# A row sum on one core: one block of 128 rows for each partition in place of two blocks of 15 and 113

## The chip, the core and the metric

The kernel runs on one core of one Trainium2 chip. The core has several engines that run side by side and wait for each other through semaphores (counters): VectorE (DVE in the profile), ScalarE (ACT), GpSimd (POOL) and SyncE (SP), which here only issues transfers. Transfers between HBM, the chip's large memory, and the core's on-chip memory with its 128 partitions are carried out by 16 DMA engines. The metric is the time of one execution on the device, in microseconds (us). The kernel before takes 160.44 us, the median of three runs (160.27 to 160.67).

## The reference

The input x has 32 x 512 rows of 1024 float32 numbers, 16384 rows and 67.1 MB in all. Each row is summed and divided by 1024:

```python
def reference(x: np.ndarray, divisor: float) -> np.ndarray:
    return (np.sum(x, axis=-1) / divisor).astype(np.float32)
```

The output is 16384 numbers, 0.07 MB. The work is reading x once.

## The kernel before

**Which partition has which rows.** With 16384 rows and 128 partitions, each partition sums J = 128 rows. The kernel divides x into two regions. The first region, the first 128 x 15 rows of x (`x_first`, F = 15), gives each partition 15 consecutive rows, so the pieces of two neighbouring partitions begin 15 rows (60 KB) apart. The second region, the rest, gives each partition W = 113 consecutive rows, which begin 113 rows (452 KB) apart. Of these 113 rows, M = 97 are called `main` (`x_main`) and L = 16 are called `last` (`x_last`). Lines 52 to 60 say this, and the same for the output.

**The loads.** A load takes some rows for all partitions at once: for each partition one contiguous piece of up to 16 rows (64 KB). The bulk loads go in turn to three buffers, `bulk0` to `bulk2`, of 16 rows each. In order they have 2, 16, 16, 16, 16, 16 and 15 rows of `main`, then the 15 rows of `first`, then the 16 rows of `last` in pieces that do not end at row boundaries: 10.625 rows and 3.66 rows into bulk buffers (loads 8 and 9), and 1.3 rows (`pa`) and 0.4 rows (`pb`) into small buffers of their own. Numbered from 0, load 6 is the 15-row one of `main` and load 7 is the one of `first`.

**Who issues them.** All transfers are issued by SP, in one queue. The first two are issued ahead of the rest (line 116). Load 2 waits for load 0 to land. From load 3 on (lines 140 to 144), load k waits until the engines have finished with load k-3, which lay in the same buffer. `pa` and `pb` follow without a wait (lines 145 and 146). Then SP waits for POOL and issues the store of the 15 results of `first` (line 148), waits for the semaphore of `pa` to reach 17, which ScalarE brings about close to the end, and issues the store of the 97 results of `main` (line 150). At the end it waits for two more signals (line 237), issues the store of the 16 results of `last` (line 238), waits for the two early stores, clears the semaphores and waits for the last store to land (line 244).

**Who sums.** VectorE reduces all rows of a load with one instruction (line 215), except in loads 6 and 7: there the table says how many rows ScalarE takes from the end of the load, 4 of 15 and 6 of 15, each with one instruction that copies a row to scratch and adds it up (line 183).

```python
    main = [(2, 0)] + [(16, 0)] * 5 + [(15, 4)]
    first = [(15, 6)]
```

The rows of `last` are shared out by hand between VectorE, which adds the two halves of a row to each other while summing (line 205), and ScalarE; both apply the division as a scale. The results of `main` and `first` are still unscaled; POOL multiplies each of the two sets with one instruction (lines 157 and 161), as soon as the loads concerned have been summed.

Of the kernel before, what the change touches and what calls it, by code (L numbers as in the profile page):

```python
# [35 lines left out]
def kernel(  # L36
# [6 lines left out]
    nc = tc.nc  # L43
    nc.at_finalize(start_loads_at_once)
    xf = x.flatten_outer_dims()
    N, D = xf.shape
    P = nc.NUM_PARTITIONS
    scale = 1.0 / float(divisor)
    J = N // P
    assert J * P == N  # L50

    F, L = 15, 16
    M = J - F - L
    W = M + L
    x_first = bass.AP(tensor=x.tensor, offset=0, ap=[[F * D, P], [1, F * D]])
    x_main = bass.AP(tensor=x.tensor, offset=P * F * D, ap=[[W * D, P], [1, M * D]])
    x_last = bass.AP(tensor=x.tensor, offset=P * F * D + M * D, ap=[[W * D, P], [1, L * D]])
    o_first = bass.AP(tensor=out.tensor, offset=0, ap=[[F, P], [1, F]])
    o_main = bass.AP(tensor=out.tensor, offset=P * F, ap=[[W, P], [1, M]])
    o_last = bass.AP(tensor=out.tensor, offset=P * F + M, ap=[[W, P], [1, L]])  # L60

    def room(name, *shape):
        return nc.alloc_sbuf_tensor(name, [P, *shape], F32).ap()
# [5 lines left out]
    bulk = [room(f"bulk{i}", 16 * D) for i in range(3)]  # L69
# [7 lines left out]
    pa, row14 = tail[:, 256 : 256 + ends[3] - ends[2]], tail[:, 255 : 256 + D - c14]  # L77
    pb = room("pb", 512)[:, : D - c15 + 2]
    part = room("part", 1)
    res0 = room("res0", F)  # L80
    res = room("res", M)
    fin = room("fin", L)
    junk = [nc.alloc_psum_tensor(f"junk{i}", [P, D], F32).ap() for i in range(4)]
# [3 lines left out]
    loads = []  # L87
    sems = {}

    def sem(name):  # L90
        sems[name] = nc.alloc_semaphore(name)
        return sems[name]

    in_bulk = [sem(f"in_bulk{i}") for i in range(3)]
    in_pa, in_pb = (sem(f"in_{n}") for n in ("pa", "pb"))
    out_first, out_main = sem("out_first"), sem("out_main")
    dve, act, pool = sem("by_dve"), sem("by_act"), sem("by_pool")
    done = sem("done")
    landed = nc.alloc_semaphore("landed")

    main = [(2, 0)] + [(16, 0)] * 5 + [(15, 4)]
    first = [(15, 6)]
    assert sum(r for r, _ in first) == F and sum(r for r, _ in main) == M
    for rows_of, src, dst in ((main, x_main, res), (first, x_first, res0)):
        j = 0
        for rows, on_act in rows_of:
            t = bulk[len(loads) % 3][:, : rows * D]
            loads.append((t, in_bulk[len(loads) % 3], src[:, j * D : (j + rows) * D], on_act, dst[:, j : j + rows]))
            j += rows
    for k in range(2):  # L110
        t = bulk[len(loads) % 3][:, : ends[k + 1] - ends[k]]
        loads.append((t, in_bulk[len(loads) % 3], x_last[:, ends[k] : ends[k + 1]], 0, None))
# [9 lines left out]
    done_dve, done_act = {}, {}  # L122
# [21 lines left out]
        nc.sync.dma_start(out=t, in_=src).then_inc(s, 16)  # L144
    nc.sync.dma_start(out=pa, in_=x_last[:, ends[2] : ends[3]]).then_inc(in_pa, 16)
    nc.sync.dma_start(out=pb[:, : D - c15], in_=x_last[:, ends[3] : ends[4]]).then_inc(in_pb, 16)
    nc.sync.wait_ge(pool, 3)
    nc.sync.dma_start(out=o_first, in_=res0).then_inc(out_first, 16)
    nc.sync.wait_ge(in_pa, 17)
    nc.sync.dma_start(out=o_main, in_=res).then_inc(out_main, 16)  # L150

# [2 lines left out]
    k = len(main) - 1  # L154
    nc.gpsimd.wait_ge(dve, done_dve[k])
    nc.gpsimd.wait_ge(act, done_act[k])
    nc.gpsimd.tensor_scalar_mul(out=res, in0=res, scalar1=scale).then_inc(pool)  # L157
    k += len(first)
    nc.gpsimd.wait_ge(act, done_act[k])
    nc.gpsimd.wait_ge(dve, done_dve[k])  # L160
    nc.gpsimd.tensor_scalar_mul(out=res0, in0=res0, scalar1=scale).then_inc(pool)  # L161


    (t8, s8, *_), (t9, s9, *_) = loads[-2:]
# [21 lines left out]
    for k, (t, s, src, on_act, dst) in enumerate(loads[:-2]):  # L186
        rows = t.shape[1] // D
# [23 lines left out]
    for k, (t, s, src, on_act, dst) in enumerate(loads[:-2]):  # L211
        m = t.shape[1] // D - on_act
        nc.vector.wait_ge(s, arrived[k])
        rows = t[:, : m * D].rearrange("p (r d) -> p r d", d=D)
# [21 lines left out]

    nc.sync.wait_ge(done, 2)
    nc.sync.dma_start(out=o_last, in_=fin).then_inc(landed, 16)
    for s in (out_main, out_first):
        nc.sync.wait_ge(s, 16)  # L240
    ids = [s.num for s in sems.values()]
    assert max(ids) - min(ids) + 1 == len(ids)
    nc.sync.sem_clear(range(min(ids), max(ids) + 1))
# [36 lines left out]
```

## Time and profile before

| what | value |
|---|---|
| median of three runs | 160.44 us |
| span of the profiled execution, first to last instruction | 159.3 us |
| time outside the span, by the median | 1.1 us |
| VectorE busy | 116.7 us (73%) |
| ScalarE busy | 18.6 us (12%) |
| POOL busy | 1.0 us (1%) |
| read from HBM | 67.11 MB, 422 GB/s over the span |
| share of the 16 DMA engines' span with packets under way | 98.1% |

The profiled execution's own time is not given apart from its span, so the median stands for it. The page of a profile lists, for each group of instructions, the engine and line, how often and how long it ran, and what ended the idle time before it. "Releaser" is what an instruction waited for last. In a timeline a line reads: start, duration, engine, line, operation, output and input with their shapes, count, and in brackets the engine's idle time before it and its releaser. A load's landing is not an instruction; it shows as the start of the first instruction that waited for it. A packet is a piece of a transfer that one DMA engine moves; a bulk load has one packet for each partition.

### The profile page before, as it was taken

Reading aid. Unit: us, or ns where it says so; the run is one execution under the profiler, and the core shown is the slowest. Engines: PE = TensorE matmul, PEld = TensorE weight load, DVE = VectorE, ACT = ScalarE, POOL = GpSimd, SP = SyncE. Lnnn points to the kernel's source line nnn. Section 1 sums busy time; section 2 is a strip of 40 time slices with the busy share of each in tenths; the row PEclk is TensorE's granted clock in tenths of the full one; section 3 lists DMA queues with packets and bytes.
Section 4 is the critical chain, followed back from the end, with each engine's and each line's share of the span. In section 5 each row is a group of like instructions: output and inputs, shape, how many; then the busy total and the mean of one; then the engine's idle time right before and its main releaser. Section 6 shows DMA issues by size and latency. Waiting matters only on the chain.

```text
span 159.3 us, 144 instructions
## 1 busy us (share of the span) xinstructions
DVE 116.7 (73%) x32; ACT 18.6 (12%) x35; POOL 1.0 (1%) x7
## 2 busy tenths in 40 slices
DVE  0500009999499994999949999499989990399296
ACT  3000000000000000000000000000009100392196
POOL 0000000000000000000000000000000001000000
DMA  8996996996996997979969969969996999889894
GB/s 296 494 527 263 527 527 263 527 527 263 527 527 263 527 444 346 527 313 477 527 263 527 527 263 527 494 278 463 494 494 262 478 494 494 350 350 525 344 401 154
DMA packets 2160, 67.18 MB, mean 422 GB/s; under 512 B 624, under 2 KB 752, under 8 KB 880
## 3 DMA queue, kind: packets, MB, share of 16 engines
q1 hardware_dynamic: 2160, 67.18, 98.1%
HBM read 67.11 MB, written 0.07 MB: 422 GB/s over the span
## 4 chain that ended last, share of the span: by engine, by line
DMA 67%; DVE 30%; another core or an unknown queue 1%; issue 0%
DMA bulk<-in_x_dram 67%; DVE res L215 29%; DVE bulk L205 1%; DVE tail L205 0%; DVE pb L205 0%; DVE fin L205 0%
## 5 line engine op out<-in xcount | busy, mean ns | idle before, releaser
L215 DVE TENSOR_REDUCE res<-bulk 128x16 f32<-128x16384 f32 (+3 forms) x8 | 110.0, 13754 | 37.7 <-DMA bulk<-in_x_dram 37.7
L183 ACT ACTIVATE junk<-bulk 128x1024 f32<-128x1024 f32 (+1 forms) x16 | 15.6, 973 | 137.2 <-DMA bulk<-in_x_dram 137.2
L205 DVE CUSTOM_DVE_ANT_0 bulk<-bulk 128x512 f32<-128x512 f32 (+1 forms) x9 | 5.5, 665 | 3.1 <-DMA bulk<-in_x_dram 3.1
L183 ACT ACTIVATION_READ_ACCUMULATOR junk<-bulk 128x1 f32 x16 | 3.0, 187 | 0.0
L183 ACT ACT_TABLE_LOAD x1 | 1.3, 1283 | 1.9 <-PEq L119 1.9
L157 POOL TENSOR_SCALAR res<-res 128x97 f32<-128x97 f32 x1 | 0.5, 465 | 129.8 <-DVE res L215 129.8
L205 DVE DVE_READ_ACCUMULATOR2_ANT fin<- 128x1 f32 x10 | 0.8, 82 | 0.0
L183 ACT ACTIVATE junk<-tail 128x737 f32<-128x737 f32 x1 | 0.8, 789 | 0.0
L205 DVE CUSTOM_DVE_ANT_0 bulk<-bulk,part 128x192 f32<-128x192 f32 x1 | 0.4, 420 | 0.3 <-DMA bulk<-in_x_dram 0.3
L205 DVE CUSTOM_DVE_ANT_0 tail<-tail 128x304 f32<-128x304 f32 x1 | 0.5, 476 | 0.0
L205 DVE CUSTOM_DVE_ANT_0 pb<-pb 128x209 f32<-128x209 f32 x1 | 0.4, 379 | 0.1
L161 POOL TENSOR_SCALAR res<-res 128x15 f32<-128x15 f32 x1 | 0.3, 262 | 15.6 <-DVE res L215 15.6
L183 ACT ACTIVATION_READ_ACCUMULATOR junk<-tail 128x1 f32 x1 | 0.2, 187 | 0.0
L153 POOL MEMSET pb<- 128x2 f32 x1 | 0.1, 99 | 1.5 <-POOLq L119 1.5
L261 POOL MEMSET const-bfloat16-1.0<- 128x1 bf16 x1 | 0.1, 101 | 0.0
L261 POOL MEMSET const-uint8-127<- 128x1 uint8 x1 | 0.1, 101 | 0.0
L261 POOL MEMSET const-float32-0.0<- 128x1 f32 x1 | 0.1, 98 | 0.2 <-issue 0.2
L261 POOL MEMSET const-float32-1.0<- 128x1 f32 x1 | 0.1, 98 | 0.0
L205 DVE DVE_READ_ACCUMULATOR2_ANT pb<- 128x1 f32 x1 | 0.1, 84 | 0.0
L205 DVE DVE_READ_ACCUMULATOR2_ANT part<- 128x1 f32 x1 | 0.1, 83 | 0.0
## 6 DMA issues: line engine op xcount, KB each, us to landing
bulk<-in_x_dram SPq DMA_DIRECT2D x2, 7680.0 KB, 39.3
bulk<-in_x_dram SPq DMA_DIRECT2D x1, 5440.0 KB, 32.0
bulk<-in_x_dram SPq DMA_DIRECT2D x1, 1872.0 KB, 23.5
bulk<-in_x_dram SPq DMA_DIRECT2D x1, 1024.0 KB, 4.6
tail<-in_x_dram SPq DMA_DIRECT2D x1, 672.0 KB, 24.7
pb<-in_x_dram SPq DMA_DIRECT2D x1, 208.0 KB, 24.8
bulk<-in_x_dram SPq DMA_DIRECT2D x5, 40.8
out_dram<-res SPq DMA_DIRECT2D x1, 48.5 KB, 1.6
```

The costliest lines, as they stand in the source:

```text
L153: nc.gpsimd.memset(pb[:, D - c15 :], 0.0).then_inc(pool)
L157: nc.gpsimd.tensor_scalar_mul(out=res, in0=res, scalar1=scale).then_inc(pool)
L161: nc.gpsimd.tensor_scalar_mul(out=res0, in0=res0, scalar1=scale).then_inc(pool)
L183: nc.scalar.activation(scratch, src, COPY, scale=by, accum_out=dst).then_inc(count)
L205: return nc.vector.tensor_tensor_reduce(out=src[:, :h], in0=src[:, :h], in1=src[:, h:], scale=by, scalar=ahead, op0=ADD, op1=ADD, accum_ou ...
L215: nc.vector.reduce_sum(out=dst[:, :m], in_=rows, axis=AX).then_inc(dve)
L261: nc = _bacc.Bacc("TRN2", target_bir_lowering=False, num_devices=1)
```

## The change

The two regions become one. Each partition owns J = 128 consecutive rows of x, and the pieces of two neighbouring partitions begin 128 rows (512 KB) apart in every load. Of the 128 rows the first M = 112 are `main` and the last L = 16 are `last`. The bulk loads of `main` have 2, then six times 16, then 14 rows; ScalarE takes 4 rows of the last 16-row load (load 6) and 5 rows of the 14-row load (load 7). The four pieces of `last` keep their sizes and their order.

With one set of 112 results there is one scaling on POOL in place of two, after load 7, and one early store in place of two. The store waits for POOL's semaphore at 2 (the clearing of two columns of `pb`, and the scaling) and then for the semaphore of `pa`, as the store of `main` did. The buffer `res0` and the semaphore `out_first` go.

```diff
-    F, L = 15, 16
-    M = J - F - L
-    W = M + L
-    x_first = bass.AP(tensor=x.tensor, offset=0, ap=[[F * D, P], [1, F * D]])
-    x_main = bass.AP(tensor=x.tensor, offset=P * F * D, ap=[[W * D, P], [1, M * D]])
-    x_last = bass.AP(tensor=x.tensor, offset=P * F * D + M * D, ap=[[W * D, P], [1, L * D]])
-    o_first = bass.AP(tensor=out.tensor, offset=0, ap=[[F, P], [1, F]])
-    o_main = bass.AP(tensor=out.tensor, offset=P * F, ap=[[W, P], [1, M]])
-    o_last = bass.AP(tensor=out.tensor, offset=P * F + M, ap=[[W, P], [1, L]])
+    L = 16
+    M = J - L
+    x_main = bass.AP(tensor=x.tensor, offset=0, ap=[[J * D, P], [1, M * D]])
+    x_last = bass.AP(tensor=x.tensor, offset=M * D, ap=[[J * D, P], [1, L * D]])
+    o_main = bass.AP(tensor=out.tensor, offset=0, ap=[[J, P], [1, M]])
+    o_last = bass.AP(tensor=out.tensor, offset=M, ap=[[J, P], [1, L]])
...
-    main = [(2, 0)] + [(16, 0)] * 5 + [(15, 4)]
-    first = [(15, 6)]
-    assert sum(r for r, _ in first) == F and sum(r for r, _ in main) == M
-    for rows_of, src, dst in ((main, x_main, res), (first, x_first, res0)):
-        j = 0
-        for rows, on_act in rows_of:
-            t = bulk[len(loads) % 3][:, : rows * D]
-            loads.append((t, in_bulk[len(loads) % 3], src[:, j * D : (j + rows) * D], on_act, dst[:, j : j + rows]))
-            j += rows
+    main = [(2, 0)] + [(16, 0)] * 5 + [(16, 4), (14, 5)]
+    assert sum(r for r, _ in main) == M
+    j = 0
+    for rows, on_act in main:
+        t = bulk[len(loads) % 3][:, : rows * D]
+        loads.append((t, in_bulk[len(loads) % 3], x_main[:, j * D : (j + rows) * D], on_act, res[:, j : j + rows]))
+        j += rows
...
-    nc.sync.wait_ge(pool, 3)
-    nc.sync.dma_start(out=o_first, in_=res0).then_inc(out_first, 16)
+    nc.sync.wait_ge(pool, 2)
     nc.sync.wait_ge(in_pa, 17)
     nc.sync.dma_start(out=o_main, in_=res).then_inc(out_main, 16)
...
-    k += len(first)
-    nc.gpsimd.wait_ge(act, done_act[k])
-    nc.gpsimd.wait_ge(dve, done_dve[k])
-    nc.gpsimd.tensor_scalar_mul(out=res0, in0=res0, scalar1=scale).then_inc(pool)
...
-    for s in (out_main, out_first):
-        nc.sync.wait_ge(s, 16)
+    nc.sync.wait_ge(out_main, 16)
```

More of the change, by code (lines that the diff above doesn't have):

```diff
@@ L79 @@
     part = room("part", 1)
-    res0 = room("res0", F)
     res = room("res", M)
@@ L95 @@
     in_pa, in_pb = (sem(f"in_{n}") for n in ("pa", "pb"))
-    out_first, out_main = sem("out_first"), sem("out_main")
+    out_main = sem("out_main")
     dve, act, pool = sem("by_dve"), sem("by_act"), sem("by_pool")
```

## The prediction

> **What bounds the kernel now.** I read the page's opening, its DMA queue and its chain first, because they say whether the time lies in transfers or in an engine.
>
> ```profile
> span 159.3 us, 144 instructions
> DVE 116.7 (73%) x32; ACT 18.6 (12%) x35; POOL 1.0 (1%) x7
> ...
> q1 hardware_dynamic: 2160, 67.18, 98.1%
> HBM read 67.11 MB, written 0.07 MB: 422 GB/s over the span
> ...
> DMA 67%; DVE 30%; another core or an unknown queue 1%; issue 0%
> ```
>
> The 16 DMA engines hold packets for 98.1% of the span, VectorE (DVE) works for 73% of it. The chain puts 30% on DVE, so the second view must say whether that share is work that the loads wait for. The timeline of DVE shows when each load had landed: the start of the instruction behind it, with the idle time before it in brackets.
>
> ```profile
> 4.61 2.29 DVE L215 TENSOR_REDUCE res<-bulk 128x2 f32<-128x2048 f32 x1 [4.61 <-DMA bulk<-in_x_dram]
> 23.93 17.22 DVE L215 TENSOR_REDUCE res<-bulk 128x16 f32<-128x16384 f32 x1 [17.04 <-DMA bulk<-in_x_dram]
> ...
> 62.65 17.22 DVE L215 TENSOR_REDUCE res<-bulk 128x16 f32<-128x16384 f32 x1 [2.15 <-DMA bulk<-in_x_dram]
> 81.98 17.22 DVE L215 TENSOR_REDUCE res<-bulk 128x16 f32<-128x16384 f32 x1 [2.11 <-DMA bulk<-in_x_dram]
> 101.57 17.22 DVE L215 TENSOR_REDUCE res<-bulk 128x16 f32<-128x16384 f32 x1 [2.38 <-DMA bulk<-in_x_dram]
> 119.83 1.03 ACT L183 ACTIVATE junk<-bulk 128x1024 f32<-128x1024 f32 x1 [116.64 <-DMA bulk<-in_x_dram]
> 119.83 11.89 DVE L215 TENSOR_REDUCE res<-bulk 128x11 f32<-128x11264 f32 x1 [1.04 <-DMA bulk<-in_x_dram]
> ...
> 137.99 9.76 DVE L215 TENSOR_REDUCE res<-bulk 128x9 f32<-128x9216 f32 x1 [6.26 <-DMA bulk<-in_x_dram]
> ...
> 150.82 0.49 DVE L205 CUSTOM_DVE_ANT_0 bulk<-bulk 128x320 f32<-128x320 f32 x1 [3.08 <-DMA bulk<-in_x_dram]
> ...
> 155.28 0.42 DVE L205 CUSTOM_DVE_ANT_0 bulk<-bulk,part 128x192 f32<-128x192 f32 x1 [0.29 <-DMA bulk<-in_x_dram]
> ```
>
> Every reduction starts because its load has landed; DVE idles 2.1 us or more before each large one. A 16-row load lands every 19.33 us at best (62.65 to 81.98), 19.59 us at worst (81.98 to 101.57): 8.39 MB in 19.33 us is 434 GB/s. And the queue never runs dry: with three buffers, SyncE (SP) issues a load when the third load before it is consumed, 17.2 us after its landing, when the load in flight has some 2 us left and a whole one stands behind it. The DVE share of the chain is the way back from a DMA issue to the reduction that freed its buffer, not a delay of the queue. So the time is the start to the first landing (4.60 us), the stream from there to 155.28 us, and a tail of 4.0 us. The last view, SP's own waits, gives the end:
>
> ```profile
> SPq L244 <- SPq L244: 0.8, 1, 0.8
> SPq L238 <- DVE fin L205: 0.6, 1, 0.6
> SPq L243 <- DMA out_dram<-res: 0.2, 1, 0.2
> ```
>
> SP waits last for the landing of the final store (0.8 us after the clear of the semaphores), and that store waits for DVE.
>
> The sum starts from the span of 159.3 us. The runs shown have a median of 160.44 (160.27 to 160.67); the 1.1 us around the span is carried unchanged, so I add changes to 160.44.
>
> **The change, part by part.**
>
> *Boundaries of the loads.* Bytes and count stay: ten bulk loads, then pa and pb. Loads 0 to 5 keep their rows. Load 6 has 16 rows for 15, so it lands one row later, 1.21 us (19.35/16), at 121.0 us. DVE reduces 12 of them instead of 11; by its two shapes (16 rows 17.22 us, 11 rows 11.89 us) a row is 1.07 us, so 12.95 us, done at 134.0 us instead of 131.7. SP issues the last bulk load (buffer 0) behind that, then pa and pb: 2.3 us later, at about 134.0, 134.4 and 134.9 us by the issue times of before. The queue needs them when the load before ends, at 150.8 us: 16 us of cover, so 0. If that cover were gone the price would be the 2.3 us. Load 7 has 14 rows for 15; the rows landed by then are 112 both times, so it lands at 138.0 us as before. DVE still takes 9 of its rows (9.76 us, done at 147.8, before the 150.8 at which it is needed); ScalarE (ACT) takes 5 instead of 6, 1.0 us less inside an idle stretch. 0.
>
> *One scaling, one early store.* The two POOL multiplications (97 columns 0.465 us, 15 columns 0.262 us) become one of 112 columns, 0.50 us by their slope, between 147.8 and 148.3 us. SP waits for it (pool at 2), then for row 14's head (in_pa at 17, met at 156.85 us): it has 8.5 us in hand, so the new order of waits delays no queued store. What goes from SP is the issue of the 15-column store at 148.2 us (0.35 us, with SP idle around it) and one wait at the end, under the landing of the last store. Its 128 packets of 60 B lay behind pb in the same queue; by the packet records each took 0.011 us, eight to an engine, 0.09 us. They write while slower engines still read pb. Saved: between 0 and 0.09 us; I take 0. The remaining early store writes 448 B a partition for 388 B: the packets of 388 B took 0.024 us, so 0.03 us more over an engine's eight packets, and the wait for that landing ends 0.8 us before the last one. 0.
>
> *The addresses.* This is what is left, and it touches every byte. Before, a load of the main part takes 64 KB from each of 128 places 452 KB apart (113 rows of 4 KB), and load 7 takes 60 KB from places 60 KB apart. After, all places of all loads are 512 KB apart, so that they agree in all lower address bits. The trace has no load at 512 KB. Its two spacings hardly differ: 18.26 us for 15 rows at 452 KB (load 6), 18.16 us at 60 KB (load 7), 1.217 and 1.211 us a row, against 1.208 in the best load. What makes the spacing matter is that the engines keep step: the packet records show the first 16 packets of 64 KB start between 3.92 and 4.24 us, the last 16 of those loads between 98.25 and 98.76 us, with each taking 2.42 us. So at any time the 16 streams stand within some 0.3 to 0.5 us, 8 to 14 KB, of the same place in their pieces; at 512 KB the streams would then fall on addresses alike but for the high bits.
>
> Bounds from the nearest rows. Between the landings at 4.60 and 155.28 lie 124.3 rows (112 less 2, and 14.28 of the last 16): 150.68 us, a mean of 1.2124 us. Low end: all at the best load's 1.2081, 0.5 us saved. High end: all at the pace of the slowest packet of 64 KB, 2.576 us where the middle one is 2.418: 1.2081 x 1.065 = 1.287 us a row, 9.3 us more. In between lie the slowest whole load, 19.59/16 = 1.2244 us, 1.5 us more, and the pace of the packet that 99 in 100 do not exceed, 2.471 us: 1.2346 us a row, 2.8 us more. I take the middle of these two, 2.1 us: a slow load is the nearest row of the same size, and a spacing that lines up all streams should make slow packets the rule. That is a choice, not a measurement.
>
> A row in the Trainium skill speaks against this change: the page "DMA: Bandwidth & Descriptors", section "Latency and other measured facts", gives copies between HBM tensors with a row pitch of 512 KiB as 207 GB/s, 214 with a padded pitch, and less at larger powers of two; by that ratio the stream would take 1.249 us a row, an estimate of 4.5 us more and 165.0 us in all. The page calls the mechanism an inference; no run here shows a pitch of 512 KB yet, and its tiles were copies of 16 KiB pieces, not loads of 64 KB.
>
> Sum: 160.44 + 0 (boundaries) + 0 (scaling and stores) + 2.1 (addresses) = **162.6 us**.
>
> **The rivals.** *The spacing does nothing* (not slower). For it: spacings of 452 and 60 KB ran within 0.6% of each other, and 90 in 100 of the 64 KB packets took at most 2.429 us, so the engines seem bound by their own pace, with room in HBM. Against it: neither spacing lines up the streams. It decides if a 16-row load lands every 19.4 us. Then 160.4 us.
>
> *The spacing bites hard.* The streams stay in step on the same part of HBM, each delayed by the others, packet after packet. For it: they start in step and are still in step after 98 us. Against it: a stream that is delayed falls behind its neighbours and so out of their way. Price: between 2.8 and 9.3 us, middle 6.1, 166.5 us. It decides from about 20 us a load (1.25 us a row, above the 1.2346). This is the case that the row of the skill's page describes, with 165.0.
>
> *The even layout is quicker.* The slow loads of before (19.59 and 18.26 us) come from where their addresses lie and vanish: all rows at 1.2081 us save 0.53 us, with the 0.09 of the store 159.8 us. For it: they are the last two of the 452 KB part. Against it: only one engine is late in them (of load 5's 16 completions 15 are in by 101.24 us, the last at 101.55), which can fall on any address. It decides if every load lands in 19.33 us.
>
> **How the numbers follow.** My forecast 0.43, bites hard 0.18, nothing 0.30, quicker 0.09. About 0.3%, 0.5 us, is what a measurement of this kernel can tell from no change. Slower is the first two, 0.61; same 0.30; faster 0.09. The range goes from 160.0, which leaves out most of the quicker case, to 166.5, which leaves out the upper half of the hard one: 0.17 out.
>
> **What would show it.** In the timeline of the changed kernel: 16-row reductions starting 19.5 to 19.8 us apart from the first to the last (right), 19.35 (nothing), above 20 (hard). DVE's idle before them grows by as much, to 2.4 us or more. Load 6's reduction has 12 rows and ends 16 us before the next-to-last bulk load lands; POOL has one multiplication of about 0.5 us near 148 us; from the last bulk landing to the end 4.0 us remain. The prediction is wrong if the tail is longer than that, if DVE stops waiting for loads, or if the rate of the loads is the same as before.

## The result and the profile after

The changed kernel takes 160.94 us (median of 22 runs, 160.37 to 161.09), the kernel before 160.36 us beside it (22 runs, 160.25 to 160.67). The ratio is 1.0029 with a 95% interval of 1.0023 to 1.0035: slower by 0.5 us, a clear difference, but a quarter of the one predicted (160.44 to 162.6 us) and right at the 0.3% that was named as the least that counts.

The page of the changed kernel, its opening and DMA queue:

```profile
span 159.7 us, 139 instructions
DVE 117.8 (74%) x32; ACT 17.6 (11%) x33; POOL 0.8 (0%) x6
...
q1 hardware_dynamic: 2016, 67.18, 98.0%
```

Nothing has changed its place: the same bytes, 144 packets fewer (the 128 of the store that is gone, and its completions), the DMA engines occupied for 98%. The timeline of VectorE, in which the start of a reduction tells when its load had landed:

```profile
4.83 2.29 DVE L204 TENSOR_REDUCE res<-bulk 128x2 f32<-128x2048 f32 x1 [4.83 <-DMA bulk<-in_x_dram]
24.12 17.22 DVE L204 TENSOR_REDUCE res<-bulk 128x16 f32<-128x16384 f32 x1 [17.00 <-DMA bulk<-in_x_dram]
43.51 17.22 DVE L204 TENSOR_REDUCE res<-bulk 128x16 f32<-128x16384 f32 x1 [2.17 <-DMA bulk<-in_x_dram]
63.29 17.22 DVE L204 TENSOR_REDUCE res<-bulk 128x16 f32<-128x16384 f32 x1 [2.56 <-DMA bulk<-in_x_dram]
82.94 17.22 DVE L204 TENSOR_REDUCE res<-bulk 128x16 f32<-128x16384 f32 x1 [2.43 <-DMA bulk<-in_x_dram]
102.23 17.22 DVE L204 TENSOR_REDUCE res<-bulk 128x16 f32<-128x16384 f32 x1 [2.07 <-DMA bulk<-in_x_dram]
121.54 12.95 DVE L204 TENSOR_REDUCE res<-bulk 128x12 f32<-128x12288 f32 x1 [2.09 <-DMA bulk<-in_x_dram]
138.51 9.75 DVE L204 TENSOR_REDUCE res<-bulk 128x9 f32<-128x9216 f32 x1 [4.01 <-DMA bulk<-in_x_dram]
151.33 0.49 DVE L194 CUSTOM_DVE_ANT_0 bulk<-bulk 128x320 f32<-128x320 f32 x1 [3.07 <-DMA bulk<-in_x_dram]
...
155.75 0.42 DVE L194 CUSTOM_DVE_ANT_0 bulk<-bulk,part 128x192 f32<-128x192 f32 x1 [0.25 <-DMA bulk<-in_x_dram]
```

The steps between the large loads are 19.39, 19.78, 19.65, 19.29 and 19.31 us. Two loads are late by 0.3 to 0.5 us, and then, from 83 us on, the loads land as quickly as the best ones of before (19.33). This is neither of the pictures in the prediction, a pace that is slow throughout or not slow at all. VectorE's idle time before the late loads is 2.56 and 2.43 us, so it waits for them, and the delay goes straight through to the end. From the last bulk landing to the end there are 159.7 - 155.75 = 4.0 us, as before.

The packet records say it more finely. They give the duration of every packet, that is, of one partition's piece on one DMA engine. Most pieces of 64 KB take 2.418 us. In the changed kernel 21 in 100 of them take over 20 ns longer, up to 2.656 us; in the kernel before 2 in 100 do. Added up over an engine, what the packets of 42 KB and more took beyond the usual best of their size (2.418 us for 64 KB) is 0.86 us after and 0.33 us before. The difference of 0.53 us is about the 0.45 us by which the two profiled spans differ. Neither profile shows a middling execution. The changed kernel's took 161.09 us, the longest of its 22. A span of 159.3 us, that of the profile before, goes with 160.6 to 160.7 us of time in the other runs, near the longest of that kernel (so 1.3 us lie outside the span, not 1.1). The profiles show what kind of loss it is, the medians how large.

### The profile page after: what moved, and what is told of

Same layout as the page of the kernel before. It is cut to its first block, busy times and chain, and to the rows that moved or that the text cites. A ratio compares the mean times of both kernels' runs of the same rounds, so it can differ in the third digit from the quotient of the medians.

```text
span 159.7 us, 139 instructions
## 1 busy us (share of the span) xinstructions
DVE 117.8 (74%) x32; ACT 17.6 (11%) x33; POOL 0.8 (0%) x6
## 4 chain that ended last, share of the span: by engine, by line
DMA 66%; DVE 30%; another core or an unknown queue 2%; ACT 1%; issue 1%
DMA bulk<-in_x_dram 66%; DVE res L204 30%; ACT junk L172 1%
## 5 line engine op out<-in xcount | busy, mean ns | idle before, releaser
L172 ACT ACTIVATE junk<-bulk 128x1024 f32<-128x1024 f32 (+1 forms) x15 | 14.6, 972 | 138.7 <-DMA bulk<-in_x_dram 138.6
L150 POOL TENSOR_SCALAR res<-res 128x112 f32<-128x112 f32 x1 | 0.5, 494 | 146.3 <-DVE res L204 146.3
```

What stands on the lines that cost most here:

```text
L172: nc.scalar.activation(scratch, src, COPY, scale=by, accum_out=dst).then_inc(count)
```

## The experiments

The theory (A): the loss comes from the addresses alone, because the 16 engines keep step and at 512 KB hinder each other. The rivals: (B) the bookkeeping, that is load sizes, the single scaling and the single early store; (C) chance, late loads that fall anywhere. This table has all runs with the median time, that of the kernel before beside it on the same chip, and the ratio, which is worked out from all times and can differ by 0.1% from the quotient of the two medians. The last two columns are worked out from the packet records of the one profile of each: how many of 100 packets of 64 KB took over 20 ns longer than 2.418 us (with halves, of 32 KB than 1.213 us), and the time lost, that is what the packets of 42 KB and more (of 32 KB with halves) took beyond the usual best of their size, summed over an engine. These columns describe the profiled execution, not the median: those of first_14 and one_p113 took 160.81 and 160.59 us, over their medians, and it shows in their 0.40 and 0.49 us lost. The row "after" is the changed kernel as first measured.

```
kernel           distance   us      before  ratio [95% interval]     slow   us lost
after            512 KB     160.94  160.36  1.0029 [1.0023, 1.0035]  21     0.86
after_again      512 KB     160.86  160.47  1.0026 [1.0017, 1.0034]  20     0.64
two_512          512 KB     161.06  160.47  1.0032 [1.0020, 1.0044]  20     0.67
after_halves     512 KB     160.94  160.35  1.0032 [1.0021, 1.0043]  12     0.70
one_p127         508 KB     160.36  160.47  1.0006 [0.9991, 1.0020]   0     0.12
one_p127_again   508 KB     160.25  160.35  1.0001 [0.9989, 1.0013]   0     0.13
one_p120         480 KB     160.32  160.45  0.9989 [0.9980, 0.9998]   0     0.12
first_14         456 KB     160.54  160.35  1.0009 [1.0001, 1.0018]   0     0.40
one_p113         452 KB     160.25  160.47  0.9988 [0.9979, 0.9997]   4     0.49
before_again     452 KB     160.45  160.45  0.9998 [0.9990, 1.0007]   0     0.09
before_halves    452 KB     160.48  160.35  1.0003 [0.9995, 1.0012]   0     0.02
one_p64          256 KB     160.45  160.45  0.9990 [0.9976, 1.0003]   1     0.14
first_two        504 KB     162.95  160.45  1.0147 [1.0128, 1.0167]   0     0.13
after_stagger    512 KB     162.43  160.35  1.0125 [1.0110, 1.0140]   3     0.62
before_stagger   452 KB     162.29  160.35  1.0114 [1.0097, 1.0131]   3     0.68
```

**Does the picture repeat?** The changed kernel without an edit.

> The changed kernel once more, unedited, to see which parts of its profile repeat. Theory A (addresses: at 512 KB the streams of the 16 engines get in each other's way at certain rows): 160.9 us, and the same two loads, those of rows 34 to 65 (loads 3 and 4), land late again, about 19.7 us apart where the others take 19.3; the first load lands at 4.8 us again. Theory C (the slow loads fall anywhere, by chance): 160.9 us, but the late loads are others this time.

The time repeats, the place of the late loads does not. The lines of its timeline:

```profile
43.50 17.22 DVE L204 TENSOR_REDUCE res<-bulk 128x16 f32<-128x16384 f32 x1 [2.26 <-DMA bulk<-in_x_dram]
63.00 17.22 DVE L204 TENSOR_REDUCE res<-bulk 128x16 f32<-128x16384 f32 x1 [2.29 <-DMA bulk<-in_x_dram]
82.40 17.22 DVE L204 TENSOR_REDUCE res<-bulk 128x16 f32<-128x16384 f32 x1 [2.18 <-DMA bulk<-in_x_dram]
101.87 17.22 DVE L204 TENSOR_REDUCE res<-bulk 128x16 f32<-128x16384 f32 x1 [2.25 <-DMA bulk<-in_x_dram]
121.27 12.95 DVE L204 TENSOR_REDUCE res<-bulk 128x12 f32<-128x12288 f32 x1 [2.17 <-DMA bulk<-in_x_dram]
```

Steps of 19.50, 19.40, 19.47 and 19.40 us, and 19.48 before them (from 24.02 us): five loads a little late in place of two very late ones, with the same fifth of the packets slow. So the rows of the late loads are not special, and the late first landing (4.83 us) is not either: it was at 4.68 us here, and at 4.6 to 4.8 us in the kernels at other distances. That part of the expectation of theory A was wrong. What repeats is the amount, here and in two more kernels at 512 KB (two_512, after_halves): so chance may say which load is late, but it is not the cause of the loss.

**Addresses or bookkeeping?** The kernel before with the addresses alone, and the changed kernel with the distance alone put back.

```diff
two_512, against the kernel before:
-    x_first = bass.AP(tensor=x.tensor, offset=0, ap=[[F * D, P], [1, F * D]])
-    x_main = bass.AP(tensor=x.tensor, offset=P * F * D, ap=[[W * D, P], [1, M * D]])
-    x_last = bass.AP(tensor=x.tensor, offset=P * F * D + M * D, ap=[[W * D, P], [1, L * D]])
+    x_first = bass.AP(tensor=x.tensor, offset=W * D, ap=[[J * D, P], [1, F * D]])
+    x_main = bass.AP(tensor=x.tensor, offset=0, ap=[[J * D, P], [1, M * D]])
+    x_last = bass.AP(tensor=x.tensor, offset=M * D, ap=[[J * D, P], [1, L * D]])
...
one_p113, against the changed kernel (127, 120 and 64 in the runs below):
-    x_main = bass.AP(tensor=x.tensor, offset=0, ap=[[J * D, P], [1, M * D]])
-    x_last = bass.AP(tensor=x.tensor, offset=M * D, ap=[[J * D, P], [1, L * D]])
+    x_main = bass.AP(tensor=x.tensor, offset=0, ap=[[113 * D, P], [1, M * D]])
+    x_last = bass.AP(tensor=x.tensor, offset=M * D, ap=[[113 * D, P], [1, L * D]])
```

> The kernel before with the addresses of the changed one alone: two parts, two scalings and two early stores, its own load sizes, but every piece 512 KB from its neighbour. Theory A (addresses): as slow as the changed kernel, 160.8 to 161.0 us, loads late at the same rows (34 to 65) and the first landing at 4.8 us. Theory B (bookkeeping: load sizes, one store, one scaling cost it): 160.3 to 160.4 us, as before.

> The changed kernel with one number edited: its pieces begin 113 rows (452 KB) apart instead of 128. Neighbouring partitions then read 15 rows in common, and the last rows of x are not read; bytes, loads, sums and stores are as in the changed kernel, the sums are those of other rows. Theory A (addresses): back to 160.3 to 160.4 us, no load over 19.6 us except by chance, first landing at 4.6 us. Theory B (bookkeeping): stays at 160.8 to 161.0 us.

Both went as theory A says in their times. With the old bookkeeping and the new addresses the time is that of the changed kernel (1.0032); with the new bookkeeping and the old distance it is 0.9988, no slower than before. (two_512 stores its results 512 B apart too, but so does one_p113, without the loss.) The timelines side by side, first two_512, with steps of 19.48, 19.67, 19.43 and 19.28 us:

```profile
24.11 17.22 DVE L215 TENSOR_REDUCE res<-bulk 128x16 f32<-128x16384 f32 x1 [17.01 <-DMA bulk<-in_x_dram]
43.59 17.22 DVE L215 TENSOR_REDUCE res<-bulk 128x16 f32<-128x16384 f32 x1 [2.26 <-DMA bulk<-in_x_dram]
63.26 17.22 DVE L215 TENSOR_REDUCE res<-bulk 128x16 f32<-128x16384 f32 x1 [2.45 <-DMA bulk<-in_x_dram]
82.69 17.22 DVE L215 TENSOR_REDUCE res<-bulk 128x16 f32<-128x16384 f32 x1 [2.21 <-DMA bulk<-in_x_dram]
101.97 17.22 DVE L215 TENSOR_REDUCE res<-bulk 128x16 f32<-128x16384 f32 x1 [2.06 <-DMA bulk<-in_x_dram]
```

and then one_p113, with 19.34, 19.38, 19.34 and 19.33 us:

```profile
24.00 17.22 DVE L204 TENSOR_REDUCE res<-bulk 128x16 f32<-128x16384 f32 x1 [17.12 <-DMA bulk<-in_x_dram]
43.34 17.22 DVE L204 TENSOR_REDUCE res<-bulk 128x16 f32<-128x16384 f32 x1 [2.11 <-DMA bulk<-in_x_dram]
62.72 17.22 DVE L204 TENSOR_REDUCE res<-bulk 128x16 f32<-128x16384 f32 x1 [2.17 <-DMA bulk<-in_x_dram]
82.06 17.22 DVE L204 TENSOR_REDUCE res<-bulk 128x16 f32<-128x16384 f32 x1 [2.12 <-DMA bulk<-in_x_dram]
101.39 17.22 DVE L204 TENSOR_REDUCE res<-bulk 128x16 f32<-128x16384 f32 x1 [2.11 <-DMA bulk<-in_x_dram]
```

Rival B is out: what the bookkeeping is worth lies within 0.1 to 0.2% of nothing.

**Which distances?** The same edit with 127, 120 and 64 rows.

> The changed kernel with its pieces 127 rows (508 KB) apart: nearly the same distance, but the starts no longer agree in their lower address bits. Neighbours share one row, so the sums of most partitions are those of other rows. Theory A in its alignment form: 160.3 to 160.4 us, as 452 KB. If only the sheer distance counts (how far the 128 places lie apart): 160.8 to 161.0 us, as 512 KB. Theory B (bookkeeping): 160.8 to 161.0 us.

> The 508 KB variant again, because its twelve times fell into two groups, eight of 160.2 to 160.7 and four of 161.0 to 161.2 us. If the second group belongs to that distance (close to 512 KB), some of the times are about 161.1 us again; if it was a passing state of that chip, all are 160.2 to 160.7 us.

> The changed kernel with its pieces 120 rows (480 KB) apart, an odd multiple of 32 KB; neighbours share 8 rows, so the sums are those of other rows. If agreement in the lower bits counts by degrees: between 160.4 and 160.8 us. If only a whole power of two lines the streams up: 160.2 to 160.4 us, as at 452 KB.

> The changed kernel with its pieces 64 rows (256 KB) apart, half the distance but a power of two as well; every row is read twice, by neighbours, and the upper half of x not at all, so the sums are those of other rows. If what counts is that the streams agree in their lower address bits: slow as at 512 KB, 160.8 to 161.2 us, with slow loads in the trace. If it takes 512 KB or more: 160.2 to 160.4 us, as at 452 KB.

At 508 and 480 KB the profiles have no slow packets of 64 KB (0 in 100), and the medians are those of 452 KB; so it is not the sheer distance. But half the power of two, 256 KB, is as quick as 452 KB too. Agreement in the lower address bits as such, which the prediction named, is not enough, though the 256 KB kernel also reads every row twice and only half of x. Of the distances tried only 512 KB is slow in the median. The 508 KB kernel kept a second group of times, 161.01 to 161.17 us in four of the first twelve and 161.19 us once in the second twelve. The kernel before was over 161 us too, but in 3 of 120 executions, all on one chip. Both profiles at 508 KB were of quick executions, so what happens in the others stays open. Nor does 512 KB cost time in every execution: 4 of the first 22 took only 160.37 to 160.56 us.

**Is the kernel before itself steady?**

> The kernel before once more, unedited, for a second profile of it. If its late load (load 5, 19.59 us) belongs to its addresses, load 5 is late again; if it fell by chance, another load or none is late. Time 160.3 to 160.5 us, ratio 1.000 within 0.1%.

Its load 5 landed 19.29 us after load 4 this time, not 19.59: the late load in the profile that the prediction was made from was chance. 64 KB packets went slow in 2 of 100 then, in 0 of 100 now, at the same median. The starts of the reductions of loads 4 and 5 in the second profile:

```profile
82.10 17.22 DVE L215 TENSOR_REDUCE res<-bulk 128x16 f32<-128x16384 f32 x1 [2.10 <-DMA bulk<-in_x_dram]
101.39 17.22 DVE L215 TENSOR_REDUCE res<-bulk 128x16 f32<-128x16384 f32 x1 [2.07 <-DMA bulk<-in_x_dram]
```

**Whose turn is slow?** Sorted by start, the packets fall into turns of 16, one for each engine. At 512 KB the slow packets gather in certain turns, where mostly 7 to 16 of the 16 are slow. In after_again the turns with a mean excess over 20 ns are numbers 0, 14, 15, 18, 19, 23, 27, 31, 35, 38, 39 and 43, counted from the first 16-row load: from 15 on, every fourth, with 14, 18 and 38 beside them. In two_512 they are four apart as well, but on other turns (8, 12, 16, 20 and 24, with more behind), so it is not always the same partitions. An engine has eight of the 128 packets of a load.

```diff
after_halves, and likewise before_halves:
+    def pieces(t, src):
+        h = 8 * D if t.shape[1] == 16 * D else t.shape[1]
+        return [(t[:, c : c + h], src[:, c : c + h]) for c in range(0, t.shape[1], h)]
...
-        nc.sync.dma_start(out=t, in_=src).then_inc(s, 16)
+        for to, of in pieces(t, src):
+            nc.sync.dma_start(out=to, in_=of).then_inc(s, 16)
```

> The changed kernel with each 16-row load issued as two transfers of 8 rows: packets of 32 KB for 64 KB, the same bytes at the same 512 KB. In the profiles at 512 KB the slow packets come in the same turn of all 16 engines, every fourth turn or so, 9.7 us apart. If that belongs to which partition's piece an engine reads (every fourth piece), the slow turns now come every 4.8 us, and the loss may grow: 160.9 to 161.6 us. If it is a rhythm in time, they stay 9.7 us apart, every eighth turn: about 160.9 us.

> The control for the run with halves: the kernel before, its 16-row loads likewise as two transfers of 8 rows. What halving itself costs or gains shows here: 160.3 to 160.7 us, with no slow turns. The address theory expects the changed kernel with halves at least 0.4 us above this one.

The address theory holds through the control: 160.94 against 160.48 us, 12 slow packets in 100 against 0. As to the rhythm, the peaks are at turns 31, 35, 39, 43, 47, 56, 60 and 63, with packets of half the size (and 66 to 68 and 72 behind them): mostly four turns apart again, now 4.9 us in place of 9.7. That points to which partition's piece is read, and against a rhythm in time; but the peaks are blurred and turns between them are slow too, so I take it as pointing only.

**Does keeping step matter?** Eight small extra transfers put half of the engines behind.

```diff
after_stagger, and likewise before_stagger:
...
             nc.sync.wait_ge(loads[0][1], arrived[0])
+            for i in range(8):
+                some = bass.AP(tensor=x.tensor, offset=8 * i * D, ap=[[D, 8], [1, D]])
+                nc.sync.dma_start(out=extra[8 * i : 8 * i + 8, :], in_=some).then_inc(in_extra, 16)
...
```

> The changed kernel with eight extra transfers of 8 partitions x 4 KB issued ahead of load 2, read from the first rows of x into a buffer that nothing uses. If each is spread over 8 of the 16 engines, these 8 fall some 1.2 us (half a packet of 64 KB) behind the other 8 for the rest of the run, so the end moves out by about 1.2 us at the most. Step theory (at 512 KB the engines hinder each other because all 16 stand near the same place of their pieces): far fewer slow packets of 64 KB than the fifth seen at 512 KB so far, under a tenth, and a time within 0.2 us of the kernel before with the same extra transfers. If the distance alone does it, in step or not: a fifth of the packets slow again and 0.4 to 0.6 us above that control.

> The control: the kernel before with the same eight extra transfers. Both theories: some 0.6 to 1.2 us above the kernel before, by the part of the delay that the rest of the queue does not even out, and less than 5 in 100 packets slow.

The starts in a turn lay 0.4 us apart before the extra transfers and 1.5 us apart after them. From there to the end of the 64 KB packets eight engines stay behind the other eight, by about 1.2 us. In the one turn that meets the extra transfers packets take up to 0.8 us longer, which is the loss of 0.62 us in the table; behind it no packet of 64 KB is slow, in any turn, at 512 KB. The timeline of after_stagger:

```profile
24.43 17.22 DVE L209 TENSOR_REDUCE res<-bulk 128x16 f32<-128x16384 f32 x1 [17.36 <-DMA bulk<-in_x_dram]
45.67 17.22 DVE L209 TENSOR_REDUCE res<-bulk 128x16 f32<-128x16384 f32 x1 [4.01 <-DMA bulk<-in_x_dram]
64.95 17.22 DVE L209 TENSOR_REDUCE res<-bulk 128x16 f32<-128x16384 f32 x1 [2.06 <-DMA bulk<-in_x_dram]
84.24 17.22 DVE L209 TENSOR_REDUCE res<-bulk 128x16 f32<-128x16384 f32 x1 [2.06 <-DMA bulk<-in_x_dram]
103.51 17.22 DVE L209 TENSOR_REDUCE res<-bulk 128x16 f32<-128x16384 f32 x1 [2.06 <-DMA bulk<-in_x_dram]
122.80 12.95 DVE L209 TENSOR_REDUCE res<-bulk 128x12 f32<-128x12288 f32 x1 [2.07 <-DMA bulk<-in_x_dram]
```

The extra transfers cost 1.9 us once (the step to 45.67 is 21.24 us, not 19.3); then the steps are 19.28, 19.29, 19.27 and 19.29, the quickest of all. The control has no slow packet behind the delay either, and steps of 19.29 and 19.30 us. The distance to its control is 0.14 us (162.43 to 162.29), with overlapping intervals, where without the delay it was 0.4 to 0.6. So at 512 KB the loss needs the engines to keep step: with half of them half a packet behind, it is gone, in four executions and the one profile. Keeping step is not enough for it: in the profile of the changed kernel the starts still lie 0.5 us apart in the last third, where 2 in 100 packets are slow. The delay itself costs more than it saves, and more than the 0.6 to 1.2 us expected.

**Versions meant to beat both.** The single scaling and load sizes of the changed kernel, with the first 2 rows, or the 14 rows of load 7, as a region of their own, so that the rest is 504 or 456 KB apart.

```diff
first_two, against the changed kernel (first_14 has F = 14, loaded as load 7, main from offset P * F * D):
+    F = 2
+    W = J - F
+    x_first = bass.AP(tensor=x.tensor, offset=0, ap=[[F * D, P], [1, F * D]])
+    x_main = bass.AP(tensor=x.tensor, offset=P * F * D - F * D, ap=[[W * D, P], [1, M * D]])
...
+    nc.sync.dma_start(out=o_first, in_=res[:, :F]).then_inc(out_first, 16)
```

> A version meant to beat both: the opening load of 2 rows becomes a region of its own (the first 2 x 128 rows of x, pieces 8 KB apart), all the rest has 126 consecutive rows a partition (504 KB apart); one scaling as in the changed kernel, two early stores. If addresses alone cost the changed kernel its time and one part's bookkeeping saves about 0.2 us (the 452 KB variant of the changed kernel took 160.25 against 160.47 us): 160.1 to 160.3 us, no load later than 19.4 us. If any large distance near 512 KB is bad: 160.8 us or more.

> A version meant to beat both: the load sizes and the single scaling of the changed kernel, but load 7 (14 rows) is a region of its own at the start of x, so that all the rest lies 114 rows (456 KB) apart; two early stores, of 98 and 14 results a partition (392 and 56 B). If the 0.1% by which the 452 and 480 KB variants of the changed kernel ran below the kernel before comes from load sizes and the single scaling: 160.25 to 160.35 us. If it came from the single early store: 160.45 us, as before.

The loads of first_two went as hoped (last bulk landing at 155.03 us, one slow packet of 64 KB among 768), and more than was hoped for was lost at the end. The DMA issues of first_two (KB, then us from issue to landing):

```profile
out_dram<-res SPq DMA_DIRECT2D x1, 55.0 KB, 4.7
out_dram<-res SPq DMA_DIRECT2D x1, 1.0 KB, 10.8
out_dram<-fin SPq DMA_DIRECT2D x1, 8.0 KB, 3.9
```

and of the kernel before, in its second profile:

```profile
out_dram<-res SPq DMA_DIRECT2D x1, 48.5 KB, 1.6
out_dram<-res SPq DMA_DIRECT2D x1, 7.5 KB, 9.4
out_dram<-fin SPq DMA_DIRECT2D x1, 8.0 KB, 1.4
```

With 8 B a partition in the first store, the two stores behind it land 3.1 and 2.5 us later than behind a store of 60 B a partition, and 6.5 us pass from the last bulk landing to the end (161.5 - 155.03) in place of 4.0. The packets of that store took 0.009 us each, so their own time is not it; what holds the landings up is open, and one run at one size shows it. first_14, with 56 B, has 1.7 and 1.4 us, as the kernel before. It was no quicker than the kernel before (1.0009); in its profile it lost 0.25 us in the 10.6-row load at 456 KB. No version beat the kernel before beyond doubt.

## Why the prediction was right or wrong

**The boundaries, at nothing: right.** Load 6's reduction of 12 rows took 12.95 us, as worked out, and ended at 134.5 us; the last loads were issued behind it, 16.8 us before the load ahead of them landed at 151.3. The 9 rows of load 7 took 9.75 us.

**One scaling, one store, at nothing: right.** POOL's multiplication took 0.494 us (0.50 predicted) and started at 148.34 us; the early store was issued at 157.41 us when the wait for the head of row 14 ended, and the tail stayed at 4.0 us. The pair two_512 and one_p113 shows it from both sides.

**The addresses, at 2.1 us: right in sign and in a part of the mechanism, wrong in size.** This is the step that failed. All of the 0.5 us is in this term; it was priced about four times too high. The sentence at fault is that a spacing that lines up the streams "should make slow packets the rule", from which I took a pace for the whole stream, between that of the slowest load and that of the packet that 99 in 100 do not exceed. At 512 KB only a fifth of the packets of 64 KB are slow, in some turns. In two of the four profiles without the extra transfers they nearly stop in the last third of those packets (2 and 8 in 100 in after and two_512); in after_again they go on (24 in 100). Of the five steps of the changed kernel only two, 19.78 and 19.65 us, lie in the 19.5 to 19.8 us that were expected of all. The mean over all packets of 64 KB was 2.431 to 2.436 us in the three kernels with such packets, 0.5 to 0.7% above 2.418, where I had put 1.3 to 2.2%. The late load of before that I leaned on was chance, so a price built on it could have come near only by luck.

That the engines keep step, and that 512 KB is slow only where they do, was argued in the prediction; after_stagger now bears it out. That the streams agree in the lower address bits is not the right condition: 256 KB agrees nearly as far and loses nothing. What 512 KB does beyond the engines, so that streams in step hinder each other, no run here shows.

**The rivals.** That the spacing does nothing would have been 160.4 us; the changed kernel lies between this and the forecast, nearer to nothing. That it bites hard did not happen. The Trainium skill's page "DMA: Bandwidth & Descriptors", section "Latency and other measured facts", gives 207 GB/s at a row pitch of 512 KiB and 214 with a padded pitch, for copies between HBM tensors. The estimate from it, 165.0 us, is not borne out for these loads: the kernel lost 0.3%, where that ratio is 3.3%. Its direction is. The quicker layout was also wrong as a whole, though something of it was seen: from 83 us on the changed kernel's loads took 19.29 to 19.31 us in the first profile of it, less than the best load of the first profile of before. The kernel before reached that pace too (19.29 us in before_again).

## What to carry to other kernels

A layout in which every partition's piece begins 512 KB from its neighbour's cost this kernel, which only streams, 0.3%; one with 256 KB cost nothing. To price such a thing, look at the packets: count how many are slow and sum their excess, rather than stretch the worst one over the whole stream. Before a late load in a single profile is taken for a property of the layout, look at a second profile of the same kernel. And a saving in bookkeeping beside a saturated queue was worth nothing here, because it did not shorten what runs after the last byte.

## What the runs showed of the hardware

- Of the distances tried between the partitions' pieces (256, 452, 456, 480, 504, 508 and 512 KB) only 512 KB had a large share of slow packets of 64 KB: 20 to 21 in 100 against 0 to 4, in one to three profiles of each. Why 256 KB is free of it is open, and so is what the long executions at 508 KB would show.
- The slow packets gather in turns of the 16 engines, often every fourth, and vanish when half of the engines lag by some 1.2 us more (0 slow packets behind the delay). Why they also nearly stop by themselves late in two of four profiles, with the engines' starts still 0.5 us apart, is open.
- Behind a store of 8 B a partition the next stores landed 2.5 to 3.1 us later than behind one of 60 B; behind one of 56 B they did not (one run with 8 B).
- Eight transfers of 32 KB in the stream cost 1.9 us (162.29 against 160.35 us in the kernel before), though they hold only 0.26 MB: 0.6 us at 434 GB/s, or 1.2 us if eight engines carry 32 KB each at the 27.1 GB/s of one (64 KB in 2.418 us).
